# First loads in halves, small loads moved behind the first block, and a split last store, in a four-stage encoder trunk

## The chip, the cores and the metric

The kernel runs on one core of one Trainium2 chip. The metric is the device time of one execution in microseconds (us). The median of three runs of the kernel before is given, and one further execution was recorded by the hardware profiler.

## The reference

Input x has 256 tokens of 1024 values; two layers follow one another, each of three steps with a normalisation behind each step:

```python
x = layer_norm(ALPHA * x + 0.5 * swiglu(x, ffn_w_in[l, 0], ffn_w_out[l, 0]), ...)
y = mlstm_mixer(x, ...)        # layer 0        (bidirectional, chunked)
y = window_attention(x, ...)   # layer 1        (16 heads, 4 key heads, ALiBi, sinks)
x = layer_norm(ALPHA * x + y, ...)
x = layer_norm(ALPHA * x + 0.5 * swiglu(x, ffn_w_in[l, 1], ffn_w_out[l, 1]), ...)
# swiglu: gu = x @ w_in (1024 x 5632); (silu(g) * u) @ w_out (2816 x 1024)
```

So there are six stages: FFN, mLSTM, FFN, FFN, attention, FFN. All data are float32.

## The kernel before, in words

**Splitting.** Every matrix product is made of three products in a faster format: each operand is written as a high part and a low part, and `mm3` adds hi x hi, hi x lo and lo x hi into one bank. For each piece of weights (128 partitions x 1024 values, 512 KB, called w_raw or s_raw while raw) ScalarE casts the high part w_hi, and VectorE subtracts to get w_lo. VectorE thus has one subtraction for each piece, beside everything else. The activations are split in the same way: `to_xT` turns x by TensorE transposes into a bank, ScalarE writes xT_hi from it and VectorE xT_lo.

**The first FFN products.** An FFN stage begins with one block of 512 columns for g and for u (8 pieces: m = 0, 1 and a = 0 to 3, two rows of 128 of the 1024 inputs in each), and then goes through GROUPS = 3 groups: four pieces "beside" (256 columns of g and of u side by side), two pieces of w_out (`down`), and then `seven`, in which a Strassen-like scheme makes eight half products out of seven. It needs sums of the turned x, S1 to S4, which `x_raw`, `x_one`, `x_two` and `x_rest` make on VectorE, ScalarE splitting each again (S_hi, S_lo). Some raw pieces (s_raw) are summed with others, by VectorE or by an accumulating load that GpSimd issues.

**The order of work.** Each engine runs its instructions in the order in which the program issues them. For the weights' splits in an FFN that order is written down by a small planner (`Paced` and `Weights.fill`), which keeps times of its own for the engines and the loads; in the mLSTM and attention stages constants say how many splits go in at each step (PU, PD, MP, TD). Raw buffers are few (RAW_BUFS = 4, and S_RAW = 6 and V_RAW = 2 while an FFN's pool is open), split buffers RING = 10. A new load goes out on SP's queue when a low part is done and its raw buffer falls free (`drop`, then `load`). All loads of x and of weights are on SP's queue, in the program's order.

**The start.** SP issues x's left half of tokens 0 to 127, the first piece, x's left half of tokens 128 to 255, the second piece, then the two right halves of x, and the other pieces. GpSimd meanwhile issues seven small loads (gcol, gw, four of gbias, sink), which are used in the mLSTM and attention stages. TensorE does 10 transposes of the identity (`warm`), turns the left half of x's first tokens, 10 more, turns the second tokens, and then starts with the first piece for both halves of the tokens. The right halves of x are turned before the second piece.

**Between stages.** `tail` ends a stage: for t in 0, 1 (128 tokens each) and o in 0, 1 (512 columns) it adds the last rows of the output product into four banks y[t][o]; `Norm` adds the residual, takes the statistics for each half and normalises. x of t = 0 is turned inside the last of the four products, x of t = 1 in the next stage: `pending()` is called there when the product of t = 0, m = 1 has come to the piece with 2 * a == PEND. The transposes need the finished x of t = 1.

**Attention.** Steps st = 0 to 10 are pipelined over the head pairs: scores(st), transposes of step st - 2, values(st - 3), and in `fill` work for TensorE that waits for nothing: parts of the q projection (QC says how far by each step) and `out_proj(c, toks)` from step 4 on, which adds the output product of head pair c for tokens 0 to 127 (t = 0) or 128 to 255 (t = 1). Before, CT = [0, 1] are done for both t at once; all others have t = 1 in the tail.

**The end.** The last stage stores x: after the last product of t = 1, o = 1, VectorE adds the residual for 512 columns, takes statistics, combines them, GpSimd computes the power -0.5, VectorE scales and shifts 512 columns at a time, and SP stores each half.

Nearly all instructions carry line 132, that of the recording helper `call`, so they are told apart by their tiles. L98 and L96 are the loads in `load`, L261 the accumulating loads, L452 to L463 the small loads and neg_sink, L531 the power in `Norm.finish`, L543 the store.

```python
def b_mm(ps, t, m, a):                                   # the first block's product
    if 4 * m + a == len(pieces):
        pieces.extend(W.take(1))
    for k in (2 * a, 2 * a + 1):
        mm3(ps, pair(xT, A, k, tok(t)), pair(pieces[4 * m + a], A, k % 2), k == 0, k == 7)
...
if t == 0 and m == 1 and 2 * a == PEND[bound[0] - 1]:     # in the FFN stages after the first
    pending()
```

Of the kernel before, what the change touches and what calls it, by code (L numbers as in the profile page):

```python
# [47 lines left out]
class Paced:  # L48
# [44 lines left out]
    def load(self, ap, source):  # L93
        if isinstance(source, list):
            for k, src in enumerate(source):
                self.nc.sync.dma_start(ap[:, k].rearrange("p (m f) -> p m f", m=src.shape[1]), src)  # L96
        else:
            self.nc.sync.dma_start(ap, source)  # L98
# [42 lines left out]
class Weights:  # L141
# [65 lines left out]

    def high(self):

        nc, i = self.nc, self.made  # L210
        p = self.plan[i]
        while self.half and (p["word"] not in self.raw or any(h[0] == p["needs"] for h in self.half)):
            self.low()
        while any(s_[0] == p["needs"] or p["word"] not in self.raw for s_ in self.sums):
            self.sum()
        if p["word"] not in self.raw:
            return False
        scale, raw = p["scale"], self.raw[p["word"]]
        hi = self.pool.tile([128, D], FR, name="w_hi", tag="w_hi", bufs=RING)
        if i == 0:  # L220
            for j in range(2):
                s_ = slice(j * 512, j * 512 + 512)
                nc.scalar.copy(hi[:, s_], raw[:, s_])
        elif scale is None:
            nc.scalar.copy(hi, raw)
        else:
            nc.scalar.activation(hi, raw, AF.Copy, scale=scale())
        self.half.append((i, hi))
        self.made += 1
        return True  # L230

    def low(self):

        nc = self.nc
        i, hi = self.half.pop(0)
        p = self.plan[i]
        k, scale, raw = p["k"], p["scale"], self.raw[p["word"]]
        lo = self.pool.tile([128, D], FR, name="w_lo", tag="w_lo", bufs=RING)
        if i == 0:
            for j in range(2):  # L240
                s_ = slice(j * 512, j * 512 + 512)
                nc.vector.tensor_sub(lo[:, s_], raw[:, s_], hi[:, s_].bitcast(F32))
        elif scale is None:
# [71 lines left out]
def trunk_kernel(ctx: ExitStack, tc: tile.TileContext, x, ffn_w_in, ffn_w_out, ln_g, ln_b, ml_w_in, ml_gate_b,  # L315
# [111 lines left out]
    def load_x(t, h):  # L427
        s_ = slice(h * 512, h * 512 + 512)
        nc.load(xt[t][:, s_], x[0, t * 128:(t + 1) * 128, s_])
# [5 lines left out]
    load_x(0, 0)  # L435
    W.load(1)
    load_x(1, 0)
    W.load(1)
    load_x(0, 1)
    load_x(1, 1)  # L440
# [11 lines left out]
    nc.gpsimd.dma_start(gcol, ml_norm_g[0].rearrange("(c p) -> p c", p=128))  # L452
    gw = consts.tile([128, 8, 16], F32, name="gw")
    nc.gpsimd.dma_start(gw, ml_w_in[0, :, 3072:3088].rearrange("(k p) g -> p k g", p=128))
    gbias = consts.tile([128, 1], F32, name="gbias")
    nc.gpsimd.memset(gbias, 0.0)
    for g in range(4):
        r = 64 * (g % 2) + 32 * (g // 2)
        nc.gpsimd.dma_start(gbias[r:r + 4], ml_gate_b[0, 4 * g:4 * g + 4].rearrange("(p o) -> p o", o=1))
    sink = consts.tile([128, 16], F32, name="sink")  # L460
    nc.gpsimd.dma_start(sink, bass.AP(tensor=at_sink.tensor, offset=at_sink.offset, ap=[[0, 128], [1, 16]]))
    neg_sink = consts.tile([128, 16], F32, name="neg_sink")
    nc.gpsimd.tensor_scalar(neg_sink, sink, -1.0, None, op0=OP.mult)  # L463
    neg_id = consts.tile([128, 128], FR, name="neg_id")
    nc.vector.tensor_scalar(neg_id, ident, -1.0, None, op0=OP.mult)
# [28 lines left out]
    def to_xT(t, src, bank, halves=range(2)):  # L494
        for h in halves:
            p = bank((128, 4, 128))
            for k in range(4):
                nc.tensor.transpose(p[:, k], src[:, (4 * h + k) * 128:(4 * h + k + 1) * 128], ident)
            split_evac(pair(xT, A, slice(4 * h, 4 * h + 4), tok(t)), p)
# [16 lines left out]
    class Norm:  # L516
        def __init__(self, t, ca, eps, gb, last=False):
            self.t, self.ca, self.eps, self.gb, self.last = t, ca, eps, gb, last
            self.stats = state.tile([128, 2, 6], F32, name="stats", tag="stats", bufs=2)

        def half(self, h, y):
            z = xt[self.t][:, h * 512:(h + 1) * 512]
            nc.vector.scalar_tensor_tensor(z, z, self.ca, y, op0=OP.mult, op1=OP.add)
            nc.vector.bn_stats(self.stats[:, h], z)

        def finish(self, spare):
            mv = state.tile([128, 2], F32, name="mv", tag="mv", bufs=2)
# [19 lines left out]
    def tail(y, h, todo, first, norm, last, turn_at, between=None):  # L547

        for t in range(2):
            for o in range(2):  # L550
                final = t == 1 and o == 1
                for n, (c, (i, w)) in enumerate(todo[t]):
                    if between is not None and t == 0 and o == 1 and n == turn_at:
                        between()
                    if final and n == turn_at:
                        emit_x(0, last)
                    mm3(y[t][o], h(c, t), pair(w, A, 0, slice(o * 512, o * 512 + 512)),
                        first and n == 0, n == len(todo[t]) - 1)
                    if final and n >= turn_at - 1:
                        W.done(i + 1, (0, 3, 0)[min(n - turn_at + 1, 2)])  # L560
# [9 lines left out]
    def ffn(l, i, n, pending, last):  # L570
        with ExitStack() as ph:
# [11 lines left out]
            if start:  # L583
                warm(10)
                to_xT(0, xt[0], ybank, (0,))
                W.split(1)
                warm(10)
                to_xT(1, xt[1], ybank, (0,))
                W.split(2)
# [13 lines left out]
            def b_mm(ps, t, m, a):  # L603
                if 4 * m + a == len(pieces):
                    pieces.extend(W.take(1))
                for k in (2 * a, 2 * a + 1):
# [25 lines left out]

            low, high = slice(0, 4), slice(4, 8)
# [15 lines left out]
            if start:  # L649
                sg = {}  # L650
                for m in range(2):
                    ps = [wbank(), wbank()]
                    for a in range(4):
                        if m == 0 and a == 1:
                            for t in range(2):
                                to_xT(t, xt[t], ybank, (1,))
                        for t in range(2):
                            b_mm(ps[t], t, m, a)
                            if m == 1 and a == 3:
                                b_mul(sg[t], ps[t])  # L660
                        early = {2: lambda: x_raw(0), 3: lambda: x_raw(1), 4: x_one, 5: x_two, 6: x_rest}
                        if 4 * m + a in early:
                            early[4 * m + a]()
                        W.done()
# [4 lines left out]
            else:  # L669
                W.open(pool, ends[bound[0]])  # L670
                for t in range(2):
                    ps = [wbank(), wbank()]
                    for m in range(2):
                        for a in range(4):
# [5 lines left out]
                            if t == 1 and a % 2:  # L680
                                [[None, lambda: x_raw(0), None, lambda: x_raw(1)], [None, x_one, None, x_two]][m][a]()
# [92 lines left out]
            for g in range(GROUPS):  # L774
                ps = [wbank(), wbank()]
                pieces = []
                for a in range(4):
                    pieces.extend(W.take(1))
                    for t in range(2):
                        for k in (2 * a, 2 * a + 1):  # L780
                            mm3(ps[t], pair(xT, A, k, tok(t)), pair(pieces[a], A, k % 2), k == 0, k == 7)
                    W.done()
# [24 lines left out]
                if g == 0 and not start:  # L807
                    x_rest()
                turn = seven(g < GROUPS - 1, unit_turn)
            nc.filler = None  # L810
# [272 lines left out]
    def attn(l, n, pending, last):  # L1083
        with ExitStack() as ph:
# [190 lines left out]
            for c in range(7):  # L1275
                fill[c + 4] = (out_proj, c, (0, 1) if c in CT else (0,))
            for st in range(11):
# [19 lines left out]
                held = [wo[c][0] for c in wo if c not in CT]  # L1297
# [13 lines left out]
            return tail(y, lambda c, t: pair(qT, A, c, tok(t)), (todo[7:], [todo[c] for c in range(8) if c not in CT]), False, norm, last, 4)  # L1311
# [43 lines left out]
```

## Time and profile before

| | |
|---|---|
| median of three runs | 941.99 us (941.48 to 942.05) |
| the profiled execution's own time | 943.43 us |
| its span, first to last instruction | 941.7 us |
| mean granted TensorE clock | 0.997 |
| instructions | 12338 |
| read from HBM | 185.68 MB, 198 GB/s over the span |

The stages begin, by the first of their matmuls, at about 7, 188, 300, 481, 669 and 756 us. A row of the timeline gives the start and the duration in us, engine, line, operation, the tile written and the tiles read, and in brackets how long the engine had been idle and what released it. The row for a matmul lasts longer than the distance to the next, since matmuls are pipelined; distances are taken between starts.

### The profile page before, as it was taken

Reading aid. Unit: us, or ns where it says so; the run is one execution under the profiler, and the core shown is the slowest. Engines: PE = TensorE matmul, PEld = TensorE weight load, DVE = VectorE, ACT = ScalarE, POOL = GpSimd, SP = SyncE. Lnnn points to the kernel's source line nnn. Section 1 sums busy time; section 2 is a strip of 40 time slices with the busy share of each in tenths; the row PEclk is TensorE's granted clock in tenths of the full one; section 3 lists DMA queues with packets and bytes.
Section 4 is the critical chain, followed back from the end, with each engine's and each line's share of the span. In section 5 each row is a group of like instructions: output and inputs, shape, how many; then the busy total and the mean of one; then the engine's idle time right before and its main releaser. Section 6 shows DMA issues by size and latency. Waiting matters only on the chain.

```text
span 941.7 us, 12338 instructions
## 1 busy us (share of the span) xinstructions
PE 924.8 (98%) x4416; PEld 764.9 (81%) x4416; DVE 799.8 (85%) x943; ACT 547.1 (58%) x781; POOL 102.8 (11%) x162
## 2 busy tenths in 40 slices
PE   8999999999999999999999999999999999999996
PEld 7788888889878778888888888887887788888885
DVE  6899998787697799988888899978878888898975
ACT  5655756347563548565535576563678554757460
POOL 2010101011111000101010101010545300000100
PEclk9999999999999999999999999999999999999998
DMA  8968773646534949685549597746543267869531
GB/s 270 358 168 315 207 271 77 214 134 208 173 110 154 308 144 331 170 326 134 178 155 341 121 331 207 254 88 202 172 143 111 68 210 260 230 217 310 161 88 45
DMA packets 98461, 187.54 MB, mean 199 GB/s; under 512 B 6720, under 2 KB 37456, under 8 KB 98400
## 3 DMA queue, kind: packets, MB, share of 16 engines
q1 hardware_dynamic: 91648, 174.09, 53.9%
q0 software_dynamic: 6752, 12.66, 8.5%
q8 instruction: 35, 0.57, 0.3%
q14 instruction: 26, 0.21, 0.1%
HBM read 185.68 MB, written 1.05 MB: 198 GB/s over the span
## 4 chain that ended last, share of the span: by engine, by line
PE 72%; DVE 12%; DMA 5%; ACT 5%; issue 3%; SPq 1%; POOL 1%; DVEq 0%; ACTq 0%; POOLq 0%
PE pw L132 45%; PE py L132 27%; DVE w_lo L132 5%; DMA s_raw<-in_ffn_w_in_dram 2%; ACT w_hi L132 2%; DMA w_raw<-in_ffn_w_in_dram 1%; DMA w_raw<-in_ffn_w_out_dram 1%; SPq L98 1%; DVE x L132 1%; DMA x<-in_x_dram 1%; ACT sc L132 1%; DVE s_raw L132 1%; DVE h L132 1%; DVE o L132 1%; SPq L96 0%
## 5 line engine op out<-in xcount | busy, mean ns | idle before, releaser
L132 DVE TENSOR_TENSOR w_lo<-w_raw,w_hi 128x1024 fp32r<-128x1024 f32 (+1 forms) x237 | 280.8, 1215 | 19.8 <-ACT w_hi L132 18.1
L132 ACT CAST w_hi<-w_raw 128x1024 fp32r<-128x1024 f32 (+1 forms) x237 | 240.8, 1049 | 79.7 <-DMA w_raw<-in_ffn_w_in_dram 24.0
L132 PE MATMUL pw<-w_hi,xT_hi 128*128 128x512 f32 x560 | 222.4, 397 | 0.3 <-ACT xT_hi L132 0.3
L132 PE MATMUL pw<-w_hi,xT_lo 128*128 128x512 f32 x560 | 218.9, 391 | 0.1
L132 PE MATMUL pw<-w_lo,xT_hi 128*128 128x512 f32 x560 | 218.5, 390 | 0.3 <-DVE w_lo L132 0.2
L132 ACT CAST w_hi<-s_raw 128x1024 fp32r<-128x1024 f32 x144 | 148.4, 1051 | 93.0 <-DVE s_raw L132 57.1
L132 DVE TENSOR_TENSOR w_lo<-s_raw,w_hi 128x1024 fp32r<-128x1024 f32 x144 | 172.5, 1219 | 18.9 <-ACT w_hi L132 18.7
L132 PE MATMUL py<-w_hi,h_hi 128*128 128x512 f32 x352 | 138.2, 393 | 0.3 <-ACT h_hi L132 0.3
L132 PE MATMUL py<-w_hi,h_lo 128*128 128x512 f32 x352 | 137.4, 390 | 0.2 <-DVE h_lo L132 0.2
L132 PE MATMUL py<-w_lo,h_hi 128*128 128x512 f32 x352 | 137.1, 390 | 0.2 <-DVE w_lo L132 0.2
L132 PEld LDWEIGHTS pw<-w_hi,xT_lo 128*128 128x128 f32 x560 | 105.1, 188 | 23.4 <-DVE xT_lo L132 0.9
L132 PEld LDWEIGHTS pw<-w_lo,xT_hi 128*128 128x128 f32 x560 | 105.3, 188 | 21.6 <-DVE w_lo L132 1.1
L132 PEld LDWEIGHTS pw<-w_hi,xT_hi 128*128 128x128 f32 x560 | 105.2, 188 | 20.8 <-ACT xT_hi L132 0.7
L132 DVE TENSOR_TENSOR s_raw<-s_raw 128x1024 f32<-128x1024 f32 x72 | 87.0, 1219 | 0.6
L261 POOL DMA_DIRECT2D s_raw<-in_ffn_w_in_dram x24 | 29.0, 1209 | 498.8 <-DVE w_lo L132 417.0
L132 PEld LDWEIGHTS py<-w_hi,h_lo 128*128 128x128 f32 x352 | 66.1, 188 | 15.2 <-DVE h_lo L132 1.4
L132 PEld LDWEIGHTS py<-w_lo,h_hi 128*128 128x128 f32 x352 | 66.1, 188 | 14.0 <-DVE w_lo L132 0.6
L132 PEld LDWEIGHTS py<-w_hi,h_hi 128*128 128x128 f32 x352 | 66.1, 188 | 13.9 <-ACT h_hi L132 0.7
L132 PE MATMUL pw<-w_hi,S_hi 128*128 128x512 f32 x192 | 74.8, 390 | 0.2 <-ACT e L132 0.2
L132 PE MATMUL pw<-w_hi,S_lo 128*128 128x512 f32 x192 | 74.7, 389 | 0.0
L132 PE MATMUL pw<-w_lo,S_hi 128*128 128x512 f32 x192 | 74.7, 389 | 0.0
L132 DVE TENSOR_TENSOR h_lo<-pw,h_hi 128x512 fp32r<-128x512 f32 x44 | 30.2, 687 | 24.8 <-ACT h_hi L132 24.7
(218 smaller groups left out, 1113.8 us busy)
## 6 DMA issues: line engine op xcount, KB each, us to landing
w_raw<-in_ffn_w_out_dram SPq DMA_DIRECT2D x88, 512.0 KB, 5.4
s_raw<-in_ffn_w_in_dram SPq DMA_DIRECT2D x72, 512.0 KB, 6.0
w_raw<-in_ffn_w_in_dram SPq DMA_DIRECT2D x56, 512.0 KB, 5.1
w_raw<-in_ffn_w_in_dram SPq DMA_DIRECT2D x96, 256.0 KB, 4.5
s_raw<-in_ffn_w_in_dram POOLq DMA_DIRECT2D x24, 512.0 KB, 6.0
w_raw<-in_ml_w_in_dram SPq DMA_DIRECT2D x24, 512.0 KB, 4.9
w_raw<-in_at_w_in_dram SPq DMA_DIRECT2D x12, 512.0 KB, 4.2
w_raw<-in_ml_w_out_dram SPq DMA_DIRECT2D x8, 512.0 KB, 4.0
```

Source lines behind the costliest of these rows:

```text
L98: self.nc.sync.dma_start(ap, source)
L132: r = f(out, *args, **kw)
L261: nc.gpsimd.dma_start(t.rearrange("p (k f) -> p k f", k=self.words[w]["k"]), v, accum_op=OP.add)
```

## The change

- x is loaded in quarters of 256 columns for the left halves and in halves for the right; the first piece is loaded and split in two halves of 128 rows (`Weights.part`), with a quarter of x between; the next two pieces are split in halves too. The products of the first two pieces follow in the order of what has come: k = 0 for both t, then two chunks of x are turned, then k = 1, then k = 2 of t = 0, then x's right halves are turned, then the rest. The second `warm` has 6 transposes in place of 10.
- The small loads, neg_sink and neg_id stand in `small_loads`, called behind the first group of the first FFN.
- The sums S1 to S4 are made at the places in XA (first FFN) and XB (the others): in the first FFN at pieces 3, 4, 4, 6, 7 in place of 2, 3, 4, 5, 6 (x_raw of the two t, x_one, x_two, x_rest); in the others at 1, 3, 4, 7, 12 in place of 1, 3, 5, 7, 12, so that only x_one moves, by one piece.
- PEND for the FFN after the mLSTM stage is 2 in place of 4: x of t = 1 is turned one piece earlier, that is 6 matmuls.
- Attention: LT = [4, 6, 11, 12, ...] says at which step `out_proj(c, (1,))` is done: c = 0 at step 4 as before, c = 1 at step 6 in place of 5, c = 2 behind the steps in place of in the tail, the others in the tail. One mm3 of the q projection moves from step 0 to step 1 (QC), PU[9] is 2 in place of 1, and TD for this stage 1 in place of 2.
- The last product (t = 1, o = 1 of the last stage) is made in two parts of 256 columns, each with its residual and statistics; the last 512 columns are shifted and stored as two parts of 256, the first of them on ScalarE's queue.

```diff
-PU = [3, 1, 2, 1, 1, 1, 1, 1, 0, 1, 1, 2]
-QC = [5, 16, 22, 27, 32]
+PU = [3, 1, 2, 1, 1, 1, 1, 1, 0, 2, 1, 2]
+QC = [5, 15, 22, 27, 32]
-CT = [0, 1]
+LT = [4, 6, 11, 12, 12, 12, 12]
+XA = [3, 4, 4, 6, 7]
+XB = [1, 3, 4, 7, 12]
+WARM = [10, 6]
-TD = [0, 3, 2, 0, 2, 2]
+TD = [0, 3, 2, 0, 1, 2]
-PEND = [6, 4, 6, 6, 6]
+PEND = [6, 2, 6, 6, 6]
...
+    def part(self, j):
+        nc, i = self.nc, self.made
+        raw, k, s_ = self.raw[self.plan[i]["word"]], self.plan[i]["k"], slice(512 * j, 512 * j + 512)
+        if j == 0:
+            self.halves = [self.pool.tile([128, D], FR, name="w" + e, tag="w" + e, bufs=RING) for e in ("_hi", "_lo")]
+        hi, lo = self.halves
+        nc.scalar.copy(hi[:, s_], raw[:, s_])
+        nc.vector.tensor_sub(lo[:, s_], raw[:, s_], hi[:, s_].bitcast(F32))
+        if j:
+            self.parts[i] = tuple(x.rearrange("p (k f) -> p k f", k=k) for x in (hi, lo))
+            self.made += 1
+            self.drop(self.plan[i]["word"])
+            self.load()
...
-    load_x(0, 0)
+    first = ffn_w_in[0, 0]
+    words[0]["src"] = [first[0:128, 0:512], lambda: load_x(1, 0, 256), first[128:256, 0:512]]
+    load_x(0, 0, 256)
     W.load(1)
-    load_x(1, 0)
+    load_x(0, 256, 512)
+    load_x(1, 256, 512)
     W.load(1)
-    load_x(0, 1)
-    load_x(1, 1)
+    load_x(0, 512, D)
+    load_x(1, 512, D)
     W.load()
...
+    def small_loads():
+        nc.gpsimd.dma_start(gcol, ml_norm_g[0].rearrange("(c p) -> p c", p=128))
+        nc.gpsimd.dma_start(gw, ml_w_in[0, :, 3072:3088].rearrange("(k p) g -> p k g", p=128))
+        nc.gpsimd.memset(gbias, 0.0)
+        for g in range(4):
+            r = 64 * (g % 2) + 32 * (g // 2)
+            nc.gpsimd.dma_start(gbias[r:r + 4], ml_gate_b[0, 4 * g:4 * g + 4].rearrange("(p o) -> p o", o=1))
+        nc.gpsimd.dma_start(sink, bass.AP(tensor=at_sink.tensor, offset=at_sink.offset, ap=[[0, 128], [1, 16]]))
+        nc.gpsimd.tensor_scalar(neg_sink, sink, -1.0, None, op0=OP.mult)
+        nc.vector.tensor_scalar(neg_id, ident, -1.0, None, op0=OP.mult)
...
-                norm[t].half(o, y[t][o])
+                for c0, c1 in ((0, 256), (256, 512)) if final and last else ((0, 512),):
+                    ...
+                    norm[t].part(o * 512 + c0, o * 512 + c1, y[t][o][:, c0:c1])
...
+            if self.last and self.t:
+                cuts = [slice(0, 512), slice(512, 768), slice(768, D)]
             for s_ in cuts:
...
-                    nc.sync.dma_start(out[0, tok(self.t), s_], z[:, s_])
+                    (nc.nc.scalar if s_.start == 512 and s_.stop < D else nc.sync).dma_start(out[0, tok(self.t), s_], z[:, s_])
...
+                        if m == 0 and 0 < a < 3:
+                            W.part(0)
+                            W.part(1)
+                        if m == 0 and a < 2:
+                            for j in range(2):
+                                for t in range(2):
+                                    b_mm(ps[t], t, m, a, (j,))
+                                    if j == t == 0 and a:
+                                        for u in range(2):
+                                            to_xT(u, xt[u], ybank, ((4, 8),))
+                                if j == 0 and not a:
+                                    for t in range(2):
+                                        to_xT(t, xt[t], ybank, ((2, 4),))
...
             for c in range(7):
-                fill[c + 4] = (out_proj, c, (0, 1) if c in CT else (0,))
+                fill[c + 4] = (out_proj, c, (0,))
...
+                for c in range(7):
+                    if LT[c] == st:
+                        out_proj(c, (1,))
+            for c in range(7):
+                if LT[c] == 11:
+                    out_proj(c, (1,))
```

More of the change, by code (lines that the diff above doesn't have):

```diff
@@ L219, in high @@
         hi = self.pool.tile([128, D], FR, name="w_hi", tag="w_hi", bufs=RING)
[L220 to L224, printed above, removed]
+        if scale is None:
             nc.scalar.copy(hi, raw)
@@ L238, in low @@
         lo = self.pool.tile([128, D], FR, name="w_lo", tag="w_lo", bufs=RING)
[L239 to L243, printed above, removed]
+        if scale is None:
             nc.vector.tensor_sub(lo, raw, hi.bitcast(F32))
@@ L551, in tail @@
                 final = t == 1 and o == 1
[L552 to L560, printed above, removed]
-                norm[t].half(o, y[t][o])
+                for c0, c1 in ((0, 256), (256, 512)) if final and last else ((0, 512),):
+                    for n, (c, (i, w)) in enumerate(todo[t]):
+                        if between is not None and t == 0 and o == 1 and n == turn_at:
+                            between()
+                        if final and n == turn_at:
+                            emit_x(0, last)
+                        mm3(y[t][o][:, c0:c1], h(c, t), pair(w, A, 0, slice(o * 512 + c0, o * 512 + c1)),
+                            first and n == 0, n == len(todo[t]) - 1, c0 > 0)
+                        if final and n >= turn_at - 1:
+                            W.done(i + 1, (0, 3, 0)[min(n - turn_at + 1, 2)])
+                    norm[t].part(o * 512 + c0, o * 512 + c1, y[t][o][:, c0:c1])
             norm[t].finish(t)
@@ L631, in x_sum, with sums_of @@
                 return f
+            def sums_of(slot):
+                for at, f in zip(XA if start else XB, (lambda: x_raw(0), lambda: x_raw(1), x_one, x_two, x_rest)):
+                    if at == slot:
+                        f()
             low, high = slice(0, 4), slice(4, 8)
@@ L806, in ffn @@
                 down(1)
-                if g == 0 and not start:
-                    x_rest()
+                if g == 0:
+                    sums_of(12)
                 turn = seven(g < GROUPS - 1, unit_turn)
+                if start and g == 0:
+                    small_loads()
             nc.filler = None
@@ L1310, in attn @@
             todo = [(c, wo[c]) for c in range(8)]
-            return tail(y, lambda c, t: pair(qT, A, c, tok(t)), (todo[7:], [todo[c] for c in range(8) if c not in CT]), False, norm, last, 4)
+            return tail(y, lambda c, t: pair(qT, A, c, tok(t)), (todo[7:], [todo[c] for c in range(8) if c == 7 or LT[c] == 12]), False, norm, last, 4)
     nc.filler = None
```

83 lines of the change are left out of this document (40 added, 43 removed).

## The prediction, made before the changed kernel ran

> **What bounds the kernel now.** I read the page's shares first, then the chain of waits, then the timeline of TensorE for every place where it stood idle, and at each of these the other engines' timelines and the loads.
>
> ```profile
> PE 924.8 (98%) x4416; PEld 764.9 (81%) x4416; DVE 799.8 (85%) x943; ACT 547.1 (58%) x781; POOL 102.8 (11%) x162
> PE 72%; DVE 12%; DMA 5%; ACT 5%; issue 3%; SPq 1%; POOL 1%; DVEq 0%; ACTq 0%; POOLq 0%
> ```
>
> TensorE is busy for 924.8 of 941.7 us, so all its idle time is about 17 us, and nothing but that, the two ends and added matmul time is at stake. The change leaves the number of products as it is but for the last one. The second line (share of the chain by engine) says that VectorE, loads and ScalarE carry parts of the chain; VectorE is saturated in some stretches, and there a piece of lead on TensorE is worth nothing. So each edit is read at its own place. The sum is made against the profiled execution, 943.43 us, which is 1.44 above the median of 941.99; I take the same difference off both. About 0.2%, 1.9 us, is what a measurement of this kernel can tell from no change.
>
> **Start.**
>
> ```profile
> 1.45 2.40 PE L132 MATMUL py<-ident 128*128 128x128 f32 x10 [1.45 <-DVE ident L132]
> ...
> 4.15 1.08 PE L132 MATMUL py<-ident,x 128*128 128x128 f32 x4 [0.30 <-DMA x<-in_x_dram]
> ...
> 5.06 1.27 PE L132 MATMUL py<-ident 128*128 128x128 f32 x10
> ...
> 6.70 0.47 PE L132 MATMUL pw<-w_hi,xT_hi 128*128 128x512 f32 x1
> ...
> 9.68 1.05 ACT L132 CAST w_hi<-w_raw 128x1024 fp32r<-128x1024 f32 x1 [2.11 <-DMA w_raw<-in_ffn_w_in_dram]
> 10.59 1.38 PE L132 MATMUL py<-ident,x 128*128 128x128 f32 x8 [0.57 <-DMA x<-in_x_dram]
> ...
> 11.72 0.47 PE L132 MATMUL pw<-w_hi,xT_hi 128*128 128x512 f32 x1
> ```
>
> The first product starts at 6.70, behind ten transposes of the identity (1.27) and two turns of four chunks. After, the turns are of two chunks, the second warming has six transposes (0.6 x 1.27 = 0.76, 0.5 less), ScalarE splits halves, and the half piece needs 256 KB less ahead of it. I put the first product at about 5.5, 1.2 earlier. The second wait is from the last matmul's issue at about 9.86 to 11.72: turning x's right halves (landed 10.59) and splitting the second piece (landed 9.68). With x's bytes the same and 6 matmuls of the second piece standing ahead of the right halves, some 0.5 to 0.7 of it goes as well. So TensorE is about 1.8 ahead at the third piece. It cannot keep all of this:
>
> ```profile
> 40.00:50.00 10.00, 10.00 (x46) 8.27 (x45) 9.97 (x12) 7.28 (x9) 0.00 (x0) 1.00 0.71 271
> ...
> 50.00:64.00 14.00, 13.84 (x63) 11.17 (x62) 13.50 (x14) 7.07 (x10) 2.51 (x2) 1.00 0.62 151
> 64.00:101.00 37.00, 37.00 (x170) 30.60 (x170) 33.72 (x34) 23.94 (x29) 0.00 (x0) 1.00 0.81 269
> ...
> 17.42 6.81 SPq L96 DMA_DIRECT2D w_raw<-in_ffn_w_in_dram  x8
> ...
> 30.03 0.44 SPq L98 DMA_DIRECT2D w_raw<-in_ffn_w_out_dram  x1
> ...
> 40.07 1.05 ACT L132 CAST w_hi<-w_raw 128x1024 fp32r<-128x1024 f32 x1 [1.62 <-DMA w_raw<-in_ffn_w_out_dram]
> ...
> 41.63 1.21 DVE L132 TENSOR_TENSOR w_lo<-w_raw,w_hi 128x1024 fp32r<-128x1024 f32 x1
> ...
> 63.73 0.50 PE L132 MATMUL py<-w_lo,h_hi 128*128 128x512 f32 x1 [0.16 <-DVE w_lo L132]
> ```
>
> In the rows of the view by windows (busy time of PE, PEld, DVE, ACT, POOL, then granted clock, DMA share, GB/s), VectorE is busy for 9.97 of 10 us and then for 13.50 of 14, up to TensorE's wait for a low part at 63.73. There the lead is what VectorE gained, not what TensorE gained. VectorE's gain is that of its loads: a raw buffer falls free when its low part is made, so the loads from 17.42 on, and the one of 30.03 that landed at 40.07, come some 1.2 earlier, as the first splits do; and the split of that piece, which now starts 41.63 - (40.07 + 1.05) = 0.51 after its high part, has that slack to give. Together 1.7. If the loads gain only half (0.6) and the slack does not close, it is 0.6 to 1.0; if TensorE's whole lead is kept, 2.4. I take **+1.7** (gain), bounds 0.6 and 2.4.
>
> Here the granted clock counts, since fewer transposes run ahead of the first product. The first ten take 2.40, the second ten 1.27: the array is at half rate until about 4, with transposes alone as work. What depends on that is a rival below.
>
> **The small loads** are issued by GpSimd right behind the accumulating loads of the first group, at about 62 to 73 us.
>
> ```profile
> q0 software_dynamic: 224, 0.08, 6.3%
> ```
>
> This is their queue in the first 12 us: 6.3% of 12 us, 0.76 us of all 16 engines. At the start that is taken from x and the weights (I count it in the 1.2 above). At 62 to 73 it lies in the row 64 to 101 above, where TensorE is busy for 37.00 of 37 us, GpSimd has issued nothing else and the DMA engines have a fifth of their time free: nothing. Without that cover it is 0.76. neg_id and neg_sink go with them: nothing.
>
> **The FFN behind the mLSTM stage.**
>
> ```profile
> 306.72 1.28 DVE L132 SCALAR_TENSOR_TENSOR x<-x,rs,ln_b 128x1024 f32<-128x1024 f32 x1
> ...
> 308.32 1.03 PE L132 MATMUL py<-ident,x 128*128 128x128 f32 x8
> ...
> 312.36 0.50 PE L132 MATMUL pw<-w_hi,xT_hi 128*128 128x512 f32 x1 [0.27 <-ACT xT_hi L132]
> ...
> 324.40 1.05 ACT L132 CAST w_hi<-s_raw 128x1024 fp32r<-128x1024 f32 x1 [2.05 <-DMA s_raw<-in_ffn_w_in_dram]
> ...
> 327.32 0.69 DVE L132 TENSOR_TENSOR S_lo<-S,S_hi 128x512 fp32r<-128x512 f32 x1 [2.50 <-ACT S_hi L132]
> ...
> 329.91 0.68 DVE L132 TENSOR_TENSOR hh<-sg,pw 128x512 f32<-128x512 f32 x1
> ...
> 330.65 0.66 PE L132 MATMUL pw<-ident,hh 128*128 128x128 f32 x4 [0.93 <-DVE hh L132]
> ```
>
> x of t = 1 is finished at 306.72 + 1.28 = 308.00, and TensorE reaches its transposes at 308.32, without a wait. Six matmuls earlier (6 x 0.226 = 1.36, spacing below) it reaches them at 306.96 and waits 1.04; behind it stand six matmuls that were done in that time before. They follow, so the wait is real, but the turned x is then ready sooner, and the 0.27 at 312.36 goes with some of the rest of that row's group: about 0.4 back. Later VectorE's order decides. hh at 329.91 already holds TensorE up by 0.93. With x_one a piece earlier, its S_lo is ready at about 326.0 in place of 327.32, but in the new order two low parts (1.2 each) come between it and the next sum, of which one stood elsewhere and one must wait for the s_raw that landed at 324.40. I get hh at about 330.86, 0.95 later. This end is fixed by a load's landing, so a delay from the transposes is absorbed ahead of it, and the two do not add up: **-0.95**, bounds 0 and -1.1.
>
> **The other FFNs.** The same new place of x_one:
>
> ```profile
> 509.21 0.68 DVE L132 TENSOR_TENSOR hh<-sg,pw 128x512 f32<-128x512 f32 x1
> 509.94 0.66 PE L132 MATMUL pw<-ident,hh 128*128 128x128 f32 x4
> ...
> 784.06 0.68 DVE L132 TENSOR_TENSOR hh<-sg,pw 128x512 f32<-128x512 f32 x1
> 785.09 0.60 PE L132 MATMUL pw<-ident,hh 128*128 128x128 f32 x4
> ```
>
> In the first, hh ends at 509.89 and TensorE uses it at 509.94, with 0.05 to spare; I work hh out 0.3 later there: **-0.3** (0 to -0.6). In the second there is 785.09 - 784.74 = 0.35 to spare: nothing.
>
> **Attention.**
>
> ```profile
> 734.35 0.74 PE L132 MATMUL pw<-pr_hi,v 128*128 128x512 f32 x2 [0.24 <-DVE pr_lo L132]
> ...
> 745.37 0.50 PE L132 MATMUL py<-w_hi,q_hi 128*128 128x512 f32 x1 [0.89 <-ACT q_hi L132]
> ...
> 753.87 1.04 PE L132 MATMUL py<-ident,x 128*128 128x128 f32 x8
> ```
>
> At 745.37 TensorE waits for the last head pair (0.89 after the end of its last busy row, 1.06 by starts). Now the six matmuls of c = 2, t = 1 (1.36) stand just ahead of it and come off the tail: the wait is filled. Of this I count 0.75: the norm of t = 0 follows that wait's end and is not earlier, so TensorE's turns of x at 753.87 gain up to 0.75 before x of t = 1 holds them. With c = 1 two steps behind c = 0, extra matmuls stand in steps 4 and 6 where ScalarE and VectorE set the pace (the wait at 734.35 is one of these): +0.3. One product of the q projection moved from step 0 to 1, PU[9] and TD move splits between steps of the same engine: nothing; their cover is VectorE's idle in those steps. **+1.05**, bounds 0.4 and 1.6.
>
> **End.**
>
> ```profile
> 695.62 0.28 PE L132 MATMUL py<-xT_hi,w_hi 128*128 128x256 f32 x1
> ...
> 697.65 0.28 PE L132 MATMUL py<-xT_hi,w_lo 128*128 128x256 f32 x1
> ...
> 932.04 0.39 PE L132 MATMUL py<-w_hi,h_hi 128*128 128x512 f32 x1
> ...
> 933.85 0.39 PE L132 MATMUL py<-w_hi,h_lo 128*128 128x512 f32 x1
> 934.28 0.69 DVE L132 SCALAR_TENSOR_TENSOR x<-x,py 128x512 f32<-128x512 f32 x1 [2.34 <-PE py L132]
> ...
> 937.37 1.41 DVE L132 SCALAR_TENSOR_TENSOR x<-x,rs,ln_b 128x512 f32<-128x512 f32 x2
> ...
> out_dram<-x SPq DMA_DIRECT2D x4, 256.0 KB, 2.0
> ```
>
> The 256-column rows are first and last of 18: 2.03 / 17 = 0.119 each. The 512-column ones are first and last of 9: 1.81 / 8 = 0.226. The last product is 18 of the latter (4.07) and becomes 36 of the former (4.28): 0.2 worse. Behind the last matmul, residual and statistics are for 256 columns in place of 512; at half of 0.69 each this saves 0.6 to 0.7. The final shift is two of 0.35, and the first of the two does not wait for the other's store; the last store carries 128 KB in place of 256 KB, for which no row of this size is there: between 0 and half of 2.0, and I take 0.25, near the end where the time does not go with the size. An issue on ScalarE's queue comes before that store and costs it nothing. **+0.55**, bounds 0.1 and 0.8.
>
> **Sum:** 1.7 - 0.95 - 0.3 + 1.05 + 0.55 = 2.05. 943.43 - 2.05 = 941.38; at the median 939.9.
>
> **The rivals.**
> *The order's losses do not appear* (B): the FFN delays are worked out from an order of instructions, not seen; if what waits there is a load that comes earlier too, both terms are 0 and the time is 939.9 - 1.25, about 938.7. For it: s_raw at 324.40 is a load, and its issue follows low parts that the start and mLSTM stages may bring forward. Against: hh already has TensorE waiting.
> *The start's lead is eaten* (C): the loads of 17.42 and after come no earlier since they are bound by bytes, and of 1.7 only 0.4 stays: 941.2. For it: DMA share 0.71 at 40 to 50 and 271 GB/s while VectorE is full.
> *The clock* (E): the array is at half rate for its first transposes (2.40 against 1.27). If with fewer of them six matmuls of the first product run at half rate (6 x 0.226 more, 1.36) with half of it hidden by waits for x, the sum loses 0.6: 940.5. The Trainium skill, "TensorE: Matmul & The Clock Gate", Part 1, says the clock rises after about 3.4 us of sustained work in a window that does not start with the kernel; by that rule a shorter warm-up can move the rise behind the first product, and so it speaks against the six transposes. The two rows of ten agree with a rise near 4 us, and TensorE's work from 1.45 on is not cut before that.
> *Slower: the store on ScalarE's queue* (D). No store of before uses that queue, so its landing is not shown. The other queue that is not SP's has this:
>
> ```profile
> gw<-in_ml_w_in_dram POOLq DMA_DIRECT2D x1, 64.0 KB, 6.9
> ```
>
> At 6.9 from issue to landing in place of 2.0 the first part would end 4.9 later than it does on SP: 939.9 + 4.9 = 944.8. It is above the 943.9 bound from a landing of about 6 us, and gives the whole gain back from 4.1. Against it: gw came in pieces of 64 bytes, among saturated loads, and at the end nothing else is on its way.
>
> **How the numbers follow.** Forecast (A) 0.47, B 0.28, C 0.11, E 0.05, D 0.06, slower by something else 0.03. A's own range is 939.2 to 940.6; two thirds of it (0.32) lie under 940.1, the bound for faster. Faster by over 0.2%: 0.32 + 0.28 = 0.60. Within: 0.15 + 0.11 + 0.05 = 0.31. Slower: 0.09. The likeliest is 939.9. The range goes from 937.6 (B with the start and attention near their upper bounds) to 941.7 (C with the end's gain lost).
>
> **What the profile after would show.** First 512-column product at 5.3 to 5.8 and no wait over 0.5 at 9 to 12; the wait before the first w_lo use near 62 longer than 0.16, and that matmul at about 62.0. q0's small loads at 62 to 73. A wait of about 1.0 for x at 307, hh near 329.2 (330.9 less the lead of 1.7), a lead of about 0.75 behind it. No wait over 0.3 where 745.37 was. Behind the last matmul some 0.9 less. Wrong, if the lead at the 63.73 product is under 0.8 (then C), if stages 2 and 3 keep all of it (B), if the early matmuls lie 0.45 apart (E), or if the store on ScalarE's queue lands after that on SP's (D).

## The result, and the profile after

The changed kernel took 954.92 us (954.2 to 956.18), the kernel before beside it 941.8. The ratio is 1.0139, 95% interval 1.0127 to 1.0151: 13.1 us slower, where 2.1 faster was forecast. The profiled execution took 955.21 us, its span 953.5.

The page of the changed kernel, the two rows that answer to the first two of the prediction:

```profile
PE 935.8 (98%) x4430; PEld 766.3 (80%) x4430; DVE 802.8 (84%) x950; ACT 547.5 (57%) x785; POOL 102.5 (11%) x162
PE 82%; DVE 7%; ACT 4%; DMA 3%; issue 2%; POOL 1%; SPq 1%; DVEq 0%; ACTq 0%; POOLq 0%
```

TensorE has 14 matmuls more (36 of 256 columns in place of 18 of 512, and four transposes fewer), but is busy for 11.0 us more (924.8 before). The span less TensorE's busy time is 17.7 us, and was 16.9: the time did not go into waits. The chain says the same: TensorE's share rises from 72 to 82%, VectorE's falls. The view by windows shows it in a stretch in which TensorE never rests. First the kernel before, then the changed one (us, then busy time and count of PE, PEld, DVE, ACT, POOL, granted clock, DMA share, GB/s):

```profile
64.00:188.00 124.00, 124.00 (x567) 102.55 (x567) 109.71 (x114) 75.36 (x91) 6.32 (x5) 1.00 0.69 220
```

```profile
64.00:188.00 124.00, 123.73 (x550) 99.97 (x549) 109.51 (x113) 73.75 (x87) 10.13 (x13) 1.00 0.71 221
```

Both are full, the granted clock is 1.00 in both, and 17 matmuls fewer got through. So each takes longer. Which ones is seen in the timeline, by the distance between starts. The first and the last row of 24 products of S, before:

```profile
66.38 0.39 PE L132 MATMUL pw<-w_hi,S_hi 128*128 128x512 f32 x1
...
71.59 0.39 PE L132 MATMUL pw<-w_hi,S_lo 128*128 128x512 f32 x1
```

and in the changed kernel, with the first and last of 18 products of xT that follow later:

```profile
66.34 0.39 PE L140 MATMUL pw<-w_hi,S_hi 128*128 128x512 f32 x1
...
71.71 0.39 PE L140 MATMUL pw<-w_hi,S_lo 128*128 128x512 f32 x1
...
82.12 0.39 PE L140 MATMUL pw<-w_hi,xT_hi 128*128 128x512 f32 x1
...
85.97 0.39 PE L140 MATMUL pw<-w_hi,xT_lo 128*128 128x512 f32 x1
```

S before: 5.21 / 23 = 0.2265 us. S after: 5.37 / 23 = 0.2335. xT after: 3.85 / 17 = 0.2265. Over the whole trace, with six distances averaged at a time, the middle value of all products with S is 0.2267 before and 0.2333 after, of all with h likewise, and of all with xT 0.2267 in both. The products with h (3 x 352) and S (3 x 192) are 1632 before (18 of them are the last product, which the changed kernel makes in parts of 256 columns); 1632 x 0.0066 = 10.8 us, about all of TensorE's added time. A single printed row doesn't show it (0.39 in both), since matmuls overlap; the mean over a group (busy time, mean ns), before and after, shows 6 ns of it:

```profile
L132 PE MATMUL pw<-w_lo,S_hi 128*128 128x512 f32 x192 | 74.7, 389 | 0.0
```

```profile
L140 PE MATMUL pw<-w_lo,S_hi 128*128 128x512 f32 x192 | 75.9, 395 | 0.0
```

What differs for h and S and not for xT is where they lie. The tile stats grew from 128 x 2 x 6 to 128 x 3 x 6, for the third part of the statistics. Its two buffers take 192 bytes of each partition in place of 128, and every tile allocated behind it moves by 64. By the addresses in the compiled programs (bytes in a partition):

```
tile     before   changed   what it is to a product
w_hi      35168     35168   the 512 columns that stream past
xT_hi    125280    125280   stationary; 90112 behind w_hi = 352 x 256
h_hi     141920    141984   stationary; 106752 = 417 x 256 before, 64 more after
S_hi     203360    203424   stationary; 168192 = 657 x 256 before, 64 more after
```

### The profile page after: what moved, and what is told of

Its sections match the earlier page's. It is cut to its first block, busy times and chain, and to the rows that moved or that the text cites. A ratio compares the mean times of both kernels' runs of the same rounds, so it can differ in the third digit from the quotient of the medians.

```text
span 953.5 us, 12378 instructions
## 1 busy us (share of the span) xinstructions
PE 935.8 (98%) x4430; PEld 766.3 (80%) x4430; DVE 802.8 (84%) x950; ACT 547.5 (57%) x785; POOL 102.5 (11%) x162
## 3 DMA queue, kind: packets, MB, share of 16 engines
HBM read 185.68 MB, written 1.05 MB: 196 GB/s over the span
## 4 chain that ended last, share of the span: by engine, by line
PE 82%; DVE 7%; ACT 4%; DMA 3%; issue 2%; POOL 1%; SPq 1%; DVEq 0%; ACTq 0%; POOLq 0%
PE pw L140 52%; PE py L140 29%; DVE w_lo L140 2%; DMA s_raw<-in_ffn_w_in_dram 2%; ACT w_hi L140 1%; DMA w_raw<-in_ffn_w_in_dram 1%; DVE x L140 1%; ACT sc L140 1%; DVE h L140 1%; SPq L106 0%; DVE o L140 0%; SPq L104 0%; ACT xT_hi L140 0%; DVE pr_lo L140 0%; DVE wt L140 0%
## 5 line engine op out<-in xcount | busy, mean ns | idle before, releaser
L140 PE MATMUL py<-w_hi,h_hi 128*128 128x512 f32 (+1 forms) x358 | 141.3, 395 | 1.0 <-ACT h_hi L140 0.5
L140 PE MATMUL py<-w_hi,h_lo 128*128 128x512 f32 (+1 forms) x358 | 140.4, 392 | 0.0
L140 PE MATMUL py<-w_lo,h_hi 128*128 128x512 f32 (+1 forms) x358 | 140.2, 392 | 0.2 <-DVE w_lo L140 0.2
L140 PEld LDWEIGHTS py<-w_hi,h_lo 128*128 128x128 f32 x358 | 67.2, 188 | 16.9 <-DVE h_lo L140 1.3
L140 PEld LDWEIGHTS py<-w_hi,h_hi 128*128 128x128 f32 x358 | 67.3, 188 | 16.9 <-ACT h_hi L140 1.4
```

Source lines behind the costliest of these rows:

```text
L140: r = f(out, *args, **kw)
```

## The experiments

The theory T: a product's distance depends on where its stationary tile starts relative to the streaming one, and 64 bytes cost it 0.0066 us. The rival O: the new order of work slows the matmuls.

| kernel | us | ratio to before | interval |
|---|---|---|---|
| before_pad64 | 952.0 | 1.0100 | 1.0085 to 1.0115 |
| after_pad64 | 953.17 | 1.0111 | 1.0095 to 1.0126 |
| before_all64 | 941.62 | 0.9990 | 0.9980 to 0.9999 |
| before_all32 | 942.2 | 0.9996 | 0.9986 to 1.0007 |
| before_stats3 | 951.92 | 1.0097 | 1.0080 to 1.0114 |
| after_pad192 | 944.05 | 1.0017 | 1.0008 to 1.0027 |
| after_pad192_places | 942.91 | 1.0007 | 0.9994 to 1.0019 |
| after_pad192_places_q | 942.47 | 1.0000 | 0.9991 to 1.0009 |
| whole_end | 942.02 | 0.9995 | 0.9986 to 1.0004 |
| before_end | 943.57 | 1.0008 | 1.0000 to 1.0017 |
| before_q | 941.88 | 0.9992 | 0.9982 to 1.0002 |
| before_attn_q | 941.1 | 0.9983 | 0.9974 to 0.9991 |

The kernel before took 942.07 beside the first four, 942.72 beside the next four and 942.09 beside the last.

**before_pad64.** The kernel before with an unused tile behind xT:

```diff
           state.tile([128, 8, S], FR, name="xT_lo", tag="xT_lo"))
+    state.tile([128, 16], F32, name="pad", tag="pad")
```

> The kernel before with one change: 64 bytes per partition are set aside behind xT_lo, so that every tile behind it (h, S, s_raw, q, kp and the rest) starts 64 bytes further on, as in the changed kernel; w_hi, w_lo and xT stay. No instruction differs. Theory T (addresses): the 1632 products of h and of S take 0.2333 in place of 0.2267 us apart, 10.9 us in all, of which waits of before may hide about 1: 951 to 953. Rival O (the new order, or more instructions, makes the matmuls slower): no change, 941.8.

952.0. No instruction differs, and the page shows 10.3 us more of TensorE for the same 4416 matmuls:

```profile
PE 935.1 (98%) x4416; PEld 766.5 (81%) x4416; DVE 802.2 (84%) x943; ACT 547.7 (58%) x781; POOL 102.7 (11%) x162
```

The distances are those of the changed kernel, 0.2333 for h and S and 0.2267 for xT. T holds; O cannot explain it.

**after_pad64.** The same line in the changed kernel, a shift of 128 in all.

> The changed kernel with 64 bytes more set aside behind xT_lo, so that h, S and the rest lie 128 bytes further on than in the kernel before, not 64. Theory T: h and S products are 0.2267 apart again and 10.9 us go: about 944, and between 939.9 and 944.3 by how much of the forecast gains is there. Rival O: no change, 955.

953.17, with 0.2325 for S and 0.2327 for h. T as written had a period of 128 bytes in it, and that is wrong: 128 off costs nearly what 64 off does.

**before_all64 and before_all32.** A tile of 64 or 32 bytes ahead of gcol (`consts.tile([128, 16], F32, name="pad")`, or 8), which moves w and all behind it.

> The kernel before with 64 bytes set aside ahead of gcol, so that all of w_hi, w_lo, xT, h and S move by 64 bytes together. Theory T1 (what counts is the place of the stationary operand relative to the moving one, modulo 128 bytes): no change, 941.8. Theory T2 (what counts is each operand's own place): the products of xT too go to 0.2333, some 3300 in all, 941.8 + 22, about 962.

> The kernel before with 32 bytes set aside ahead of gcol: w_hi, w_lo, xT, h and S all start at a multiple of 128 bytes, with no difference between them. T1: no change, 941.8 (perhaps 1 either way, since other tiles, such as q and kp, move relative to what they stood by). T2: another spacing than 0.2267 for all of them, in either direction; a gain of 0.0067 each would give about 920, a loss 962.

941.62 and 942.2, and 0.2267 for xT, h and S in both. So T1: it is the place of one tile relative to the other. An operand's own place, at 32, 96 or 0 modulo 128, did not matter.

**before_stats3.** The tile stats as wide as in the changed kernel, in the kernel before, its third part unused:

```diff
-            self.stats = state.tile([128, 2, 6], F32, name="stats", tag="stats", bufs=2)
+            self.stats = state.tile([128, 3, 6], F32, name="stats", tag="stats", bufs=2)
...
-            nc.vector.bn_aggr(mv, self.stats)
+            nc.vector.bn_aggr(mv, self.stats[:, 0:2])
```

> The kernel before with one number changed: the tile stats is 128 x 3 x 6 in place of 128 x 2 x 6, its third part unused, as the changed kernel makes it. Its two buffers then take 192 bytes in place of 128, and everything behind moves by 64. Theory T: 952, as with 64 bytes set aside. Rival: 942.

```profile
PE 935.5 (98%) x4416; PEld 766.4 (81%) x4416; DVE 802.3 (84%) x943; ACT 547.5 (58%) x781; POOL 103.0 (11%) x162
```

951.92, where the kernel before took 942.72 beside it: the wider tile alone makes 9.2 us of the loss.

**after_pad192.** The changed kernel with an unused tile of 48 values, a shift of 256 in all.

> The changed kernel with 192 bytes set aside behind xT_lo: h, S and the rest lie 256 bytes further on than in the kernel before. A shift of 128 had left their products at 0.2333 us. Theory T256 (the stationary tile must start at the same place as the moving one modulo 256 bytes): 0.2267 again, PE's busy time 10.9 us less, so about 942 to 944, and 939.9 if every gain of the forecast is there. Rival O (something else of the change holds these products up): 953 to 955.

```profile
PE 925.1 (98%) x4430; PEld 765.6 (81%) x4430; DVE 800.8 (85%) x950; ACT 546.8 (58%) x785; POOL 103.7 (11%) x162
```

944.05, TensorE 10.7 us less, 0.2267 again. The remaining parts of the change are seen here without the shift: 0.17% slower, where 0.22% faster was forecast.

**after_pad192_places.** As above, with two constants as before: `PEND = [6, 4, 6, 6, 6]` and `XB = [1, 3, 5, 7, 12]`.

> The changed kernel with 192 bytes set aside, and with x_one at piece 5 and the turn of x (t = 1) at piece 4 in the FFN behind the mLSTM stage, as before. By the forecast's steps the waits of about 1 us at the transposes of x near 308 and of 0.3 more at hh go: 1.25 faster than the changed kernel with 192 bytes set aside alone. Rival B (those losses are not real in time, the engines give the same back later): no difference between the two, within 0.5.

942.91, 1.1 less. The intervals of the two meet (0.0010 between the ratios), so the time alone doesn't settle it. The waits, in after_pad192:

```profile
307.67 1.09 PE L140 MATMUL py<-ident,x 128*128 128x128 f32 x8 [0.95 <-DVE x L140]
...
330.67 0.65 PE L140 MATMUL pw<-ident,hh 128*128 128x128 f32 x4 [0.99 <-DVE hh L140]
...
510.63 0.66 PE L140 MATMUL pw<-ident,hh 128*128 128x128 f32 x4 [0.65 <-DVE hh L140]
```

The first is the wait for x of t = 1 that the forecast put at 1.04; with PEND = 4 it isn't there. The last two are the waits for hh: 0.99 where before had 0.93, and 0.65 where before had none. But the second doesn't go with x_one. In after_pad192_places, with x_one back at piece 5, it is longer:

```profile
509.67 0.66 PE L140 MATMUL pw<-ident,hh 128*128 128x128 f32 x4 [0.91 <-DVE hh L140]
```

**after_pad192_places_q and before_q.** In the attention stage of the kernel before q lies 160 bytes off w modulo 256, as in after_pad192_places, and its products with w have 0.2333 in both. One line moves q, kp and v by 96:

```diff
             pool = ph.enter_context(tc.tile_pool(name="attn", bufs=1))
+            pool.tile([128, 24], F32, name="qpad", tag="qpad", bufs=1)
```

> The same, and with 96 bytes set aside at the start of the attention pool, so that q_hi, q_lo, kp and v start at the place of w_hi modulo 256 bytes (before, 160 off). Theory T256: the 96 products of w with q there go from 0.2333 to 0.2267, 0.6 us, and kp by q as well if it counts for them: 0.6 to 1.0 faster than without. Rival (only tiles of the same row of the ring count, not the class modulo 256): no difference, and 0.2333 stays in the trace.

> The kernel before with 96 bytes set aside at the start of the attention pool and nothing else: q, kp and v there start at the place of w_hi modulo 256 bytes. Theory T256: 96 products 0.0067 closer, 0.6 faster than before. Rival: waits of attention take it back, no change.

The distance of these products goes to 0.2267 in after_pad192_places_q, as T says. In before_q the middle value is 0.2283, with the ten or so behind a wait further apart and 0.2267 after them (746.39 to 751.83 in 24 distances); in before_attn_q, below, it is 0.2267. Those of kp by q stay at 0.23. The times, 0.9993 of the kernel without it in the changed one and 0.9992 on its own, have the expected sign and size, but 0.6 us is within their intervals.

**before_attn_q.** before_q with LT, QC, PU and TD of the change and the code for LT.

> The same as before_q, with the attention part of the change (LT, QC, PU, TD) and none of its other parts. By the forecast 1.05 faster than before_q (0.4 to 1.6); the trace of the changed kernel shows about 0.85 between the start of that stage and the next. Rival: VectorE's splits, moved between the steps, take it back: no difference from before_q.

941.1, 0.0009 less than before_q by the ratio (0.8 us). The wait of 0.90 for the last q_hi, in before_q:

```profile
743.97 0.50 PE L132 MATMUL py<-w_hi,q_hi 128*128 128x512 f32 x1 [0.90 <-ACT q_hi L132]
```

is gone; in before_attn_q the first and the last of 44 products, 9.74 / 43 = 0.2265 apart, with no gap:

```profile
742.22 0.39 PE L132 MATMUL py<-w_hi,q_hi 128*128 128x512 f32 x1
...
751.96 0.39 PE L132 MATMUL py<-w_lo,q_hi 128*128 128x512 f32 x1
```

From the first product of kp by q to the first of S in the next FFN it is 117.38 us in before_q and 116.12 here: 1.26 gained. With 0.9983 (0.9974 to 0.9991) this is the clearest gain of the study. How little 0.001 means is seen in before_all64, which changes no instruction and has 0.9980 to 0.9999.

**before_end.** Class Norm and `tail` of the changed kernel in the kernel before, with 192 bytes set aside.

> The kernel before with only the split end of the changed one (192 bytes set aside, so that h and S stay in their class modulo 256 bytes). By the trace: 0.9 slower than before. By the forecast: 0.55 faster.

1.0008 (1.0000 to 1.0017): slower at the edge of its interval, with the sign that the trace of the changed kernel had shown. TensorE, VectorE and the stores in before_end:

```profile
931.10 0.28 PE L132 MATMUL py<-w_hi,h_lo 128*128 128x256 f32 x1
931.90 0.39 PE L132 MATMUL py<-w_hi,h_hi 128*128 128x256 f32 x1 [0.52 <-DVE x L132]
```

```profile
931.42 0.42 DVE L132 SCALAR_TENSOR_TENSOR x<-x,py 128x256 f32<-128x256 f32 x1 [0.41 <-PE py L132]
...
934.35 0.42 DVE L132 SCALAR_TENSOR_TENSOR x<-x,py 128x256 f32<-128x256 f32 x1 [2.05 <-PE py L132]
```

```profile
out_dram<-x SPq DMA_DIRECT2D x3, 256.0 KB, 2.1
out_dram<-x ACTq DMA_DIRECT2D x1, 128.0 KB, 2.1
out_dram<-x SPq DMA_DIRECT2D x1, 128.0 KB, 2.0
```

The second half's first product waits until VectorE has read the first half out of the same bank: 0.80 from start to start in place of 0.12. Whether the chip or only the program's semaphores ask for this wait was not tried. The 128 KB stores land after 2.0 and 2.1 us, as the 256 KB ones do. From the start of the last product to the end of the program it was 11.7 us before (933.85 less 17 x 0.2267 is 930.0; end 941.7) and is 12.8 here (929.07 to 941.9). Of the 1.1 between them, 0.43 lies behind the landing of the last store: from there to the end it was 0.90 before and is 1.34 here. SP ends each program with waits for semaphores, two at a time and in a fixed order, about 0.06 us each. These are the ones from the last store's landing on, before and in before_end (the count, then ns):

```profile
L1351 SPq EVENT_SEMAPHORE  x1: 28/28/28, 940.8 to 940.8; - x1
```

```profile
L1358 SPq EVENT_SEMAPHORE  x8: 28/28/28, 940.5 to 941.0; - x8
```

Before, the last store's semaphore stood in the last of these waits. In before_end seven follow it, in after_pad192 four (1.15 us to the end).

**whole_end.** after_pad192_places_q with the last product and its store whole.

> The changed kernel with its places (192 bytes behind xT_lo, 96 at the attention pool) and with x_one and the turn of x as before, and now also with the last product, its residual, its shift and its store whole, as before. By the trace of the two ends (a wait of 0.67 of the second half for VectorE's reading of the first, stores of 128 KB that land no sooner than those of 256 KB) the split costs 0.9: about 941.5 beside 942.4 with the split. By the forecast it gained 0.55: 943.0.

942.02, 0.0005 below the split by the ratio: the sign of the trace, not clear of the interval. By the traces, from the first product of S in the last FFN to the end, it is 137.50 us with the split and 136.95 here; before had 136.65. The last 0.3 is SP's waits behind the last store's landing again (1.20 in place of 0.90 to the end). whole_end also holds the start and the small loads beside what before_attn_q has, and is not faster than that one: of the start no gain arrives that these times can show. The start was not run by itself.

## Why the prediction was wrong, point by point

**The step that failed** is in its second paragraph: that only idle time, the two ends and added matmul time were at stake, and with it the fixed distance of 0.226 for every product of 512 columns. Distances were taken from the trace of before and used for a program whose tiles lie elsewhere. The wider stats tile was priced at nothing, since it is no work. It cost most of the 13.1 us: 9.2 by itself in the kernel before (951.92 against 942.72), and 10.9 came back when its shift was undone in the changed kernel (954.92 to 944.05). None of the rivals had it either. A sum over waits could not have found it. The two numbers that could were there beforehand: the addresses of both programs, and in the trace of before the products of q at 0.2333 beside those of xT at 0.2267.

**Start (+1.7).** The first product came at 5.59 (5.5 was forecast), but in this execution the wait behind it stayed:

```profile
4.19 1.42 PE L140 MATMUL py<-ident 128*128 128x128 f32 x6
...
5.59 0.48 PE L140 MATMUL pw<-w_hi,xT_hi 128*128 128x512 f32 x1
...
8.69 0.41 PE L140 MATMUL py<-ident,x 128*128 128x128 f32 x2 [0.93 <-DMA x<-in_x_dram]
```

This is the second quarter of x for tokens 128 to 255, now the sixth load to go out; before, it was part of the third. The other five profiles with the new start have one such wait of over 0.5 (0.51). TensorE's lead at the third piece was put at 1.8, and that was too much: the 25th product of 512 columns starts at 14.7 in the mean of the six profiles with the old start and h a multiple of 256 bytes from w, and at 13.9 in that of the four with the new start and h so placed. Executions differ here by 1 to 2 us: the transposes of e that follow the first products of S start at 73.8 to 75.6 in the six (mean 74.4) and at 72.9 to 73.7 in the four (73.3). So 1.1 is gained by there, for 1.7 forecast. Then 0.75 is lost: from those transposes to the mLSTM's first product of gw it is 125.3 to 125.4 us with the old start and 126.1 to 126.2 with the new one. The place, in after_pad192, TensorE and ScalarE, and then ScalarE before:

```profile
170.98 0.50 PE L140 MATMUL py<-w_hi,h_hi 128*128 128x512 f32 x1 [0.28 <-ACT h_hi L140]
```

```profile
169.40 1.04 ACT L140 CAST w_hi<-w_raw 128x1024 fp32r<-128x1024 f32 x1
170.34 0.59 ACT L140 CAST h_hi<-pw 128x512 fp32r<-128x512 f32 x1
```

```profile
169.02 1.05 ACT L132 CAST w_hi<-w_raw 128x1024 fp32r<-128x1024 f32 x1 [1.60 <-DMA w_raw<-in_ml_w_in_dram]
...
170.59 0.58 ACT L132 CAST h_hi<-pw 128x512 fp32r<-128x512 f32 x1
```

In the last group of that FFN the high part of a later piece now stands ahead of h_hi; before, it stood ahead of g, where ScalarE was idle. Which of the edits to the first FFN makes this order was not tried. The prediction followed the order of work to 64 us and took the rest as unchanged. The small loads at nothing stand: no wait came with them.

**FFN behind the mLSTM (-0.95) and the next (-0.3).** The wait of 1.04 for x came as 0.95 in after_pad192 and is gone with the places undone; so far the mechanism is right. Whether it cost time is open. 1.1 us came back (1.25 was forecast), within the intervals, but from the first product of xT to the first of S in this FFN it is 50.96 us in after_pad192, and 49.4 to 51.0 in the nine profiles with h so placed and the old places. The loss at hh, on which the forecast rested, is not shown: its wait in this FFN runs from none to 1.42 in these nine. In the next FFN (0.3 forecast) the wait of 0.65 is 0.91 and 0.78 in two of the three kernels with the new start and x_one back at piece 5, none in the third, and none in the six with the old start. What makes it stays open.

**Attention (+1.05).** Right: 1.26 by the trace, 0.8 by the times.

**End (+0.55).** Wrong in sign: 0.9 lost in after_pad192 (12.6 us from the start of the last product to the end, 11.7 before), 1.1 in before_end. Up to the last store's landing it is 0.6 in both. In before_end the matmuls took 1.12 more from first to last start (4.97 against 3.85), where 0.2 was forecast; the second half's wait for VectorE on the shared bank is 0.68 of it and was in no term. The shorter residual and statistics gave 0.65, as forecast. The shift in three instructions took 0.15 more, and the smaller store, priced at 0.25, saved nothing (2.03 us from issue to landing, as before). The rest, 0.25 and 0.43, is in SP's waits behind the landing, which were in no term either.

**The rivals.** D did not happen: ScalarE's queue landed its store in 2.1 us, not 6.9. E did not: the six transposes ran at half rate (1.42, where ten took 1.27), but the first two distances behind them, 0.52 and 0.34, are those of before (0.53 and 0.34), and from the third on the products were 0.23 apart (6.45 to 7.14 in four rows). Here the trace does not show the harm that the rule of the Trainium skill, "TensorE: Matmul & The Clock Gate", Part 1, allowed. C holds for the most part, by another way than it said: the lead was there, smaller than forecast, and was lost in an order. B is not settled: the wait for x is there, its price is not shown.

**Sum without the shift.** Start 0.3, attention 1.0 and end -0.9 come to +0.4, and to -0.7 if the FFNs' 1.1 is all a loss, where after_pad192 measured 0.17% (0.8 to 2.5 us) slower. So even then 0.1 to 1.8 is not placed.

## What to carry to other kernels

A tile that holds no data of a matmul can still slow it, by moving others: compare the start addresses of stationary and streaming tiles of two programs, and the distance between matmul starts for each pair of operands, before pricing anything by a duration from the old trace. Splitting a last product in one bank let the reader of the first half hold up the second half's matmuls. A lead gained early has to be followed through every order that depends on it, as far as a wait that sets the pace.

## What the runs showed of the hardware

For 512 columns, a product's distance was 0.2267 us where the stationary tile starts a multiple of 256 bytes from the streaming tile, and 0.2325 to 0.2333 at every other place that was run: 64 and 128 off (h and S), and 32, 160 and 224 off (q). Moving both together by 32 or 64 changed nothing. For 256 columns it was the other way round. These are the first and the last start of the first half of the last product, in the changed kernel (h 64 off) and in after_pad192 (a multiple of 256):

```profile
941.10 0.28 PE L140 MATMUL py<-w_hi,h_hi 128*128 128x256 f32 x1
...
943.03 0.28 PE L140 MATMUL py<-w_hi,h_lo 128*128 128x256 f32 x1
```

```profile
929.69 0.28 PE L140 MATMUL py<-w_hi,h_hi 128*128 128x256 f32 x1
...
931.73 0.28 PE L140 MATMUL py<-w_hi,h_lo 128*128 128x256 f32 x1
```

1.93 / 17 = 0.1135 us at 64 off and 2.04 / 17 = 0.1200 at a multiple of 256; at 128 off (after_pad64) it was 0.1188. So the place that is best for 512 columns is not best for every product.

Other offsets were not run, nor is it shown why; that the period is 256 and not something that 256 happens to meet rests on h, S, xT and q at differences of 0 and 256 modulo 512. No wait, no granted clock and no single row's duration shows it; the starts do, and the mean over a large group of one shape.
